# Strassen's seven block products for gate and up, and the down projection as a phase of its own, in a two-layer diffusion backbone

## Chip, cores and metric

One NeuronCore of a Trainium2 chip. The metric is the device time of one execution in microseconds (us), the median of several runs.

## What is computed

Two layers over 1024 latent tokens and 256 context tokens, width 1024. Each layer normalizes its input, mixes tokens (windowed attention, a Fourier mix, a gated linear attention), projects out, and then runs a SwiGLU feed-forward network (FFN). The change concerns the FFN of the latent tokens:

```python
def swiglu(h, w_ffn_in, w_ffn_out):
    gate, up = jnp.split(h @ w_ffn_in, 2, axis=-1)
    return (jax.nn.silu(gate) * up) @ w_ffn_out

        x = x + gt1 * (mix @ w_out[l])
        h2 = rms_norm(x, g_norm2[l]) * (1.0 + sc2) + sh2
        x = x + gt2 * swiglu(h2, w_ffn_in[l], w_ffn_out[l])
```

The hidden width is 2816, 22 inner tiles of 128 (`FT`). Everything is float32.

## The kernel before

Activations lie with features on the partitions: a `[128, 8, 512]` tile holds the 1024 features (eight blocks, `KT`) of one half of the latent tokens (half 0, half 1). To keep float32 precision at the fast matmul rate, every operand is split in a high part (a cast, ScalarE) and the rest (a subtraction, VectorE): `split`, lines 160 to 162. A product then takes three matmuls (`mm3`, lines 164 to 168: high x high, high x low, low x high), and `gemm` (lines 170 to 174) sums eight blocks in one PSUM bank: 24 matmuls of 128x512. `load_w` (line 143) loads a weight tile of 512 KB into one of two `raw` buffers and splits it into one of three `wh` and three `wl` buffers.

The code is written as generators that `weave` (line 71) runs in turn, each with its pace in `PACE`; a framework then orders each engine's queue by the order of the code and by which operands it expects to be ready, and inserts all semaphores. Loads and stores are issued from SP's queue. An engine's queue is worked off in order.

`lat_early` (line 1106) projects half 0 out, normalizes it, and in layer 1 does its first FFN blocks beside the rest of the attention; `lat_late` (line 1082) does the same for half 1. In the norm (`norm_stats` line 379, `norm_apply_g` line 401) each block of 128 features takes one VectorE step, one ScalarE step that writes the high part, and one VectorE step that writes the low part. The norm of half 1 is cut in two (`self.mid`): gate and up of half 0 of the first block stand between its statistics and its application.

The FFN (`ffn_lat`, line 1190) goes in 11 blocks of two inner tiles (`FB`). `ffn_up` makes gate and up of both halves of a block: 96 matmuls per inner tile; the gate goes through Silu (line 1125), the up result is multiplied by it (line 1138), the product is split and stays on the chip. `ffn_down` (line 1165) follows one block later: for each half and each of the eight output blocks six matmuls into one bank, whose result is scaled and added into the half's `x` (line 1178). Every inner tile's down weights are loaded and split once and used for both halves. Between the blocks of layer 0 stand seven rows each of the next layer's modulation (`next_mod`, line 1046): a row is a 512 KB load into a `raw` buffer and one VectorE multiply-and-sum (line 326). In layer 1 the first `F0` = 2 blocks of half 0 are done early, and those of half 1 at the end.

Of the kernel before, what the change touches and what calls it, by code (L numbers as in the profile page):

```python
# [8 lines left out]
F32 = mybir.dt.float32  # L9
# [14 lines left out]
F0 = 2  # L24
# [17 lines left out]
class Prog:  # L42
# [55 lines left out]
    def run(self):  # L98
# [17 lines left out]
        self.mid = None  # L116
# [47 lines left out]
    def mm3(self, ps, wh, wl, xh, xl, start, stop):  # L164
        mm = self.nc.tensor.matmul
        mm(ps, wh, xh, start=start, stop=False)  # L166
        mm(ps, wh, xl, start=False, stop=False)  # L167
        mm(ps, wl, xh, start=False, stop=stop)  # L168
# [249 lines left out]
    def layer(self, l):  # L418
# [9 lines left out]
        with tc.tile_pool(name=f"mix{l}", bufs=2, reuse_waits="tile") as mp:  # L428
# [12 lines left out]
            self.ch, self.pend, self.joint = {}, None, True  # L441
# [604 lines left out]
    def next_mod(self, l, pool):  # L1046
        nc = self.nc
        cs = {}
        for s, n in (("c", 16), ("l", 48)):
            cs[s] = self.t(pool, [128, 1024], F32, "cs", 1)  # L1050
# [10 lines left out]
    def lat_load(self, l, c, x, pool, tag):  # L1061
        act = self.act_tiles(pool, tag, 8, 2, 512)
# [4 lines left out]
        self.ch[c] = (act, x, pool, tag)  # L1067

    def lat_proj(self, l, c):
        act, x = self.ch[c][:2]  # L1070
        for m in range(KT):
# [3 lines left out]
            self.nc.vector.scalar_tensor_tensor(x(m), ps, self.mods[l, "l", 0][2][:, m:m + 1], x(m), ALU.mult, ALU.add)  # L1075
            yield 5.1

    def lat_late(self, l, x):
        self.lat_load(l, 1, x, self.fp, "H2")
        yield PACE[f"late{l}"]  # L1080
        yield from self.lat_proj(l, 1)
        yield from self.wait((l, "early"))
        if not self.f0:
            for z in range(2):
                self.prefetch("wff1", l, 0, z)
        self.mid = self.lat_norm_g(l, 1)
        next(self.mid)

    def lat_norm(self, l, c):
        for _ in self.lat_norm_g(l, c):  # L1090
            pass

    def lat_norm_g(self, l, c):
        n = 512
        _, x, pool, tag = self.ch[c]
        a2, sh2, _ = self.mods[l, "l", 1]
        h2 = self.act_tiles(pool, tag, 8, 2, n)
        nr = self.norm_stats(self.resident(x, n), n, False)
        yield
        self.norm_apply(self.resident(x, n), n, nr, a2, sh2, h2, False)  # L1100
        self.ch[c] = (h2, x)

    def lat_early(self, l, x, f0):
        self.lat_load(l, 0, x, self.bp, "H")
        yield 10
        yield from self.lat_proj(l, 0)
# [3 lines left out]
        self.lat_norm(l, 0)  # L1110
        self.emitted.add((l, "early"))
        yield 10
        if f0:
            yield from self.ffn_steps(l, [(b, [0]) for b in range(f0)], False, self.mm_ps)

    def ffn_up(self, l, b, cs, table, tag=("nx", 3)):
        nc = self.nc
        gs = {}

        def gate(c, w):  # L1120
            ps = self.mm_ps()
            self.gemm(ps, w, self.ch[c][0])
            sg = self.t(self.tp, [128, 512], F32, *tag)[:]
            if table:
                i = nc.scalar.activation(sg, ps, ACTF.Silu)
                self.last_silu = i.ins
            else:
                raw = self.t(self.tp, [128, 512], F32, *tag)[:]
                nc.scalar.copy(raw, ps)
                nc.scalar.activation(sg, ps, ACTF.Abs)  # L1130
                self.silu_tail(raw, sg)
                nc.vector.tensor_tensor(sg, raw, sg, ALU.mult)
            return sg

        def up(f, c, w, sg):
            ps = self.mm_ps()
            self.gemm(ps, w, self.ch[c][0])
            nc.vector.tensor_tensor(sg, ps, sg, ALU.mult)  # L1138
            if c == 0:
                g = self.t(self.bp, [128, 2, 512], F32R, "HC", 4)  # L1140
            else:
                g = self.t(self.fp, [128, 2, 512], F32R, "G", 4)
            self.split(sg, g[:, 0, :], g[:, 1, :])
            gs[f, c] = g

        ld = lambda f, z: self.load_w("wff1", l, b * FB + f, z)
        for f in range(FB):
            wg = ld(f, 0)
            wu = ld(f, 1)
            if not self.joint:  # L1150
                for c in cs:
                    if c and self.mid:
                        next(self.mid, None)
                        self.mid = None
                    sg = gate(c, wg)
                    up(f, c, wu, sg)
                self.joint = len(cs) > 1
            else:
                sgs = [gate(c, wg) for c in cs]
                for c, sg in zip(cs, sgs):  # L1160
                    up(f, c, wu, sg)
            yield 10.2 * len(cs)
        self.pend = (b, cs, gs)

    def ffn_down(self, l, psum):
        nc = self.nc
        b, cs, gs = self.pend
        gt2 = self.mods[l, "l", 1][2]
        w2 = [self.load_w("wff2", l, b * FB + f) for f in range(FB)]
        for c in cs:  # L1170
# [193 lines left out]
```

## Time and profile before

| | |
|---|---|
| median of 3 runs (range) | 3077.03 us (3073.91 to 3078.86) |
| profiled execution | 3071.83 us |
| its span, first to last instruction | 3069.9 us |
| mean granted TensorE clock | 0.966 |
| layer 0, first to last FFN gate or down projection | about 988 to 1722 us |
| layer 1, the same | about 2310 to 3067 us |

Times of rows are in us from the span's start, mean durations in ns. PE is TensorE, PEld its weight loads, DVE VectorE, ACT ScalarE, POOL GpSimd, SPq the queue of SP that issues DMAs. Matmuls are pipelined: the duration of one is longer than the distance of two starts. PEclk 1.00 is a granted clock of 2.4 GHz, 0.50 is 1.2 GHz. A row "x2" in a timeline is two instructions merged, from the start of the first to the end of the second.

### The profile page before, as it was taken

How to read it: one execution, taken by the hardware profiler on the slowest of the kernel's cores; microseconds unless marked ns; L12 is line 12 of the kernel's file. 1: busy time of each engine (PE TensorE's matmuls, PEld its weight loads, DVE VectorE, ACT ScalarE, POOL GpSimd, SP SyncE). 2: the span in 40 equal slices, each digit the busy share in tenths (PEclk: the TensorE clock that was granted, in tenths of full speed). 3: DMA queues.
4: the chain of work that ended last, by engine and by line, in shares of the span. 5: the costliest groups of instructions: out<-in, count | busy, mean ns of one | idle time of the engine just before them, and what ended most of it. 6: DMA issues, size and time to landing. Idle time of an engine off the chain costs nothing. (4 is left out here: it accounts for less than half of the span.)

```text
span 3069.9 us, 37102 instructions
## 1 busy us (share of the span) xinstructions
PE 2885.3 (94%) x14450; PEld 2316.7 (75%) x14450; DVE 1762.0 (57%) x2857; ACT 1137.8 (37%) x2064; POOL 79.4 (3%) x72
## 2 busy tenths in 40 slices
PE   6999997979989999999999998895999999999999
PEld 3577676868877888888888866664667888888887
DVE  4266778787766555444445677776665533334434
ACT  3356565555544211121112465454444311111111
POOL 0000100000000000000000000010100000000000
PEclk9999997989999999999999999995999999999999
DMA  7754452434562333332322434233342111111113
GB/s 249 255 159 137 117 163 72 131 100 155 182 202 93 110 120 106 103 110 96 114 85 96 154 121 145 86 121 110 107 134 90 62 55 49 48 48 48 42 63 109
DMA packets 156847, 349.35 MB, mean 114 GB/s; under 512 B 19136, under 2 KB 54720, under 8 KB 155648
## 3 DMA queue, kind: packets, MB, share of 16 engines
q1 hardware_dynamic: 156672, 346.98, 35.4%
q8 instruction: 114, 1.87, 0.2%
q14 instruction: 61, 0.50, 0.1%
HBM read 306.27 MB, written 38.02 MB: 112 GB/s over the span
## 5 line engine op out<-in xcount | busy, mean ns | idle before, releaser
L166 PE MATMUL mm<-H,wh 128*128 128x512 f32 x2080 | 821.4, 396 | 12.6 <-ACT HC L408 3.8
L167 PE MATMUL mm<-H,wh 128*128 128x512 f32 x2080 | 818.9, 395 | 1.3 <-DVE H L162 1.3
L168 PE MATMUL mm<-H,wl 128*128 128x512 f32 x2080 | 816.8, 393 | 0.9 <-DVE wl L162 0.9
L161 ACT CAST wh<-raw 128x1024 fp32r<-128x1024 f32 (+1 forms) x332 | 341.5, 1038 | 913.1 <-PE mm L167 473.9
L162 DVE TENSOR_TENSOR wl<-raw,wh 128x1024 fp32r<-128x1024 f32 (+1 forms) x332 | 401.7, 1218 | 389.7 <-ACT wh L161 382.6
L166 PEld LDWEIGHTS mm<-H,wh 128*128 128x128 f32 x2080 | 392.1, 189 | 102.1 <-issue 5.5
L167 PEld LDWEIGHTS mm<-H,wh 128*128 128x128 f32 x2080 | 392.6, 189 | 85.1 <-issue 2.6
L168 PEld LDWEIGHTS mm<-H,wl 128*128 128x128 f32 x2080 | 392.6, 189 | 85.1 <-issue 3.3
L1138 DVE TENSOR_TENSOR nx<-mm,nx 128x512 f32<-128x512 f32 x86 | 59.4, 690 | 202.1 <-PE mm L168 201.7
L166 PE MATMUL mm<-HC,wh 128*128 128x256 f32 (+1 forms) x560 | 166.3, 298 | 2.2 <-DVE dcol L795 1.4
L167 PE MATMUL mm<-HC,wh 128*128 128x256 f32 (+1 forms) x560 | 163.5, 293 | 0.9 <-DVE HC L409 0.6
L168 PE MATMUL mm<-HC,wl 128*128 128x256 f32 (+1 forms) x560 | 161.6, 290 | 0.8 <-DVE wl L162 0.8
L167 PE MATMUL f<-G,wh 128*128 128x512 f32 x352 | 136.9, 389 | 0.0
L166 PE MATMUL f<-G,wh 128*128 128x512 f32 x352 | 136.6, 389 | 0.3 <-DVE XA L1178 0.3
L168 PE MATMUL f<-G,wl 128*128 128x512 f32 x352 | 136.8, 389 | 0.0
L326 DVE CUSTOM_DVE_ANT_0 na<-raw,cs 128x1024 bf16<-128x1024 f32 x64 | 78.3, 1224 | 100.8 <-DMA raw<-wmodT 100.8
L166 PE MATMUL f<-HC,wh 128*128 128x512 f32 x336 | 131.2, 390 | 1.0 <-DVE XA L1178 1.0
L669 ACT ACTIVATE P<-S,nm 128x640 f32<-128x640 f32 (+2 forms) x144 | 104.7, 732 | 71.4 <-DVE nm L665 70.8
L167 PE MATMUL f<-HC,wh 128*128 128x512 f32 x336 | 130.8, 389 | 0.0
L168 PE MATMUL f<-HC,wl 128*128 128x512 f32 x336 | 130.6, 389 | 0.0
L691 PE MATMUL t<-ident,P 128*128 128x128 f32 x640 | 110.4, 288 | 12.1 <-DVE pt L696 4.8
L663 DVE TENSOR_REDUCE mx<-S 128x2 f32<-128x1280 f32 (+2 forms) x68 | 95.7, 1407 | 40.8 <-PE S L658 40.4
(441 smaller groups left out, 4465.0 us busy)
## 6 DMA issues: line engine op xcount, KB each, us to landing
raw<-wff SPq DMA_DIRECT2D x216, 512.0 KB, 3.3
raw<-wmodT SPq DMA_DIRECT2D x64, 512.0 KB, 3.6
raw<-wfm SPq DMA_DIRECT2D x52, 512.0 KB, 3.9
raw<-wout SPq DMA_DIRECT2D x40, 512.0 KB, 3.3
pt<-wmod SPq DMA_DIRECT2D x64, 256.0 KB, 4.5
qld<-q_l SPq DMA_DIRECT2D x64, 256.0 KB, 4.3
raw<-wtm SPq DMA_DIRECT2D x24, 416.0 KB, 3.7
wm<-wmod SPq DMA_DIRECT2D x8, 1024.0 KB, 9.6
```

What stands on the lines that cost most here:

```text
L161: self.nc.scalar.copy(hi, raw)
L162: (eng or self.nc.vector).tensor_tensor(lo, raw, hi.bitcast(F32), ALU.subtract)
L166: mm(ps, wh, xh, start=start, stop=False)
L167: mm(ps, wh, xl, start=False, stop=False)
L168: mm(ps, wl, xh, start=False, stop=stop)
L326: self.nc.vector.tensor_tensor_reduce(out=junk[:], in0=raw, in1=cs[s][:], op0=ALU.mult, op1=ALU.add, scale=1.0, scalar=0.0, accum_out=self ...
L663: nc.vector.tensor_reduce(mx[:, :nh], st[:, c0:c0 + nh * n].rearrange("p (a n) -> p a n", n=n), axis=AX.X, op=ALU.max)
L669: nc.scalar.activation(P[:, :n], st[:, c0 + z * n:c0 + (z + 1) * n], ACTF.Exp, bias=nm[:, hh:hh + 1], accum_out=sums[:, hh:hh + 1])
L691: nc.tensor.transpose(tp[:, hh * 128:(hh + 1) * 128], P[:, c:c + 128], self.ident[:])
L1138: nc.vector.tensor_tensor(sg, ps, sg, ALU.mult)
```

## The change

Gate and up of both halves of one inner tile are a 2 x 2 block product: weights G1, G2 and U1, U2 (the first and last four blocks of the inner dimension) times operands B11, B21 (half 0) and B12, B22 (half 1). `ffn_seven` makes it from seven products of four blocks each in place of eight. Five of its operand sets are sums or differences of the normalized halves, made and split once per layer (`combo`, `combos2`); five of the seven weight operands are sums made per inner tile on GpSimd and then split. The products run three ahead in weights, into four banks per tile, two banks taking a second product after the first has been read. The gated results go to DRAM (`gd`). The norm now writes a float32 tile in place and the split follows apart (`norm_raw`). The output projection's `x` goes to DRAM (`xm`) as well.

The down projection then is a phase by itself: for each half, 22 inner tiles, eight PSUM banks that collect all of them, each inner tile with a load of its weights (now once for each half) and of its gated result. In layer 0 the next layer's norm of half 0 stands behind the first three (`LAG`) inner tiles of half 1, which use six banks. `F0` counts inner tiles now: in layer 1 six are done in the plain way, half 0 early and half 1 ahead of `ffn_seven`, gate and up only. `next_mod` gives three rows after each of layer 0's tiles.

The diff, cut:

```diff
-F0 = 2
+F0 = 6
+FS = ("F", 20)
+LAG = 3
...
+    def norm_raw(self, l, x):
+        nr = self.norm_stats(self.resident(x, 512), 512, False)
+        for k in (4, 5, 6, 7, 0, 1, 2, 3):
+            nc.vector.scalar_tensor_tensor(x(k), x(k), a2[:, k:k + 1], nr, ALU.mult, ALU.mult)
+            nc.scalar.activation(x(k), x(k), ACTF.Identity, bias=sh2[:, k:k + 1])
...
+    def lat_late(self, l):
...
+        yield from self.lat_proj(l, 1, act, x)
+        yield from self.wait((l, "early"))
+        self.norm_raw(l, x)
+        self.raw1 = x
+        B = self.B
+        B["22"] = self.half(self.fp, FS)
+        for k in range(4):
+            self.split(x(k + 4), *B["22"](k))
+        if self.f0:
+            B["12"] = self.half(self.fp, FS)
+            for k in range(4):
+                self.split(x(k), *B["12"](k))
+        r = self.raw0
+        self.combo("1+", self.fp, FS, lambda k: (r(k), x(k + 4), ALU.add))
+        self.combo("4-", self.fp, FS, lambda k: (r(k + 4), r(k), ALU.subtract))
+
+    def combo(self, name, pool, tag, parts):
+        self.B[name] = self.half(pool, tag)
+        for k in range(4):
+            a, b, op = parts(k)
+            t = self.t(self.tp, [128, 512], F32, "nx", 3)[:]
+            (self.nc.vector if "+" in name else self.nc.gpsimd).tensor_tensor(t, a, b, op)
+            self.split(t, *self.B[name](k))
+
+    def combos2(self):
+        r, x = self.raw0, self.raw1
+        self.combo("3-", self.bp, ("H", 8), lambda k: (x(k), x(k + 4), ALU.subtract))
+        self.combo("7+", self.fp, FS, lambda k: (r(k + 4), x(k + 4), ALU.add))
+        for k in range(4):
+            self.nc.vector.tensor_tensor(r(k), r(k), x(k), ALU.add)
+        self.B["6+"] = self.half(self.fp, FS)
+        for k in range(4):
+            self.split(r(k), *self.B["6+"](k))
...
+    def ffn_seven(self, l, fs, fps):
...
+        def weights(i):
+            f, p = fs[i // 7], i % 7
+            if p == 0:
+                g = self.t(self.wp, [128, 1024], F32, "raw", 2)
+                u = self.t(self.bp, [128, 1024], F32, "XC", 2)
+                for z, w in ((0, g), (1, u)):
+                    nc.sync.dma_start(w[:], self.wff1[l, f, z].rearrange("p a b -> p (a b)"))
+                raws[f] = g, u
+            g, u = raws[f]
+            g1, g2, u1, u2 = g[:, 0:512], g[:, 512:1024], u[:, 0:512], u[:, 512:1024]
+            pair = [(u1, u2, ALU.add), (g1, g2, ALU.add), (g1, u2, ALU.add), u2, g1,
+                    (g2, u2, ALU.subtract), (u1, g1, ALU.subtract)][p]
+            if isinstance(pair, tuple):
+                src = self.t(self.tp, [128, 512], F32, "c1", 2)[:]
+                nc.gpsimd.tensor_tensor(src, *pair)
             else:
+                src = pair
...
+            self.split(src, w[:, 0, :], w[:, 1, :])
+            ws[i] = w
+
+        ops = ["11", "22", "1+", "4-", "3-", "7+", "6+"]
+        ev = self.t(self.bp, [128, 8, 512], F32, "XA", 1)
...
+            T1, T2, T3, T4 = [ev[:, 4 * (j % 2) + z, :] for z in range(4)]
+            for p in range(7):
+                i = 7 * j + p
+                if i + ahead < n:
+                    weights(i + ahead)
+                w, b = ws.pop(i), B[ops[p]]
+                ps = bank[(0, 1, 2, 0, 1, 2, 3)[p]]
...
+                    self.mm3(ps, w[:, 0, ks], w[:, 1, ks], xh, xl, first and k == 0, k == 3, skip)
+                if p == 0:
+                    nc.scalar.copy(T1, ps)
+                elif p == 1:
+                    tt(T2, T1, ps, ALU.add)
+                elif p == 2:
+                    tt(T3, ps, T2, ALU.subtract)
+                elif p == 3:
+                    nc.scalar.copy(T4, ps)
+                    tt(T2, T4, T2, ALU.subtract)
+                elif p == 4:
+                    self.last_silu = nc.scalar.activation(T1, ps, ACTF.Silu).ins
+                    tt(T3, ps, T3, ALU.add)
+                elif p == 5:
+                    tt(T2, ps, T2, ALU.add)
+                    self.last_silu = nc.scalar.activation(T2, T2, ACTF.Silu).ins
+                    tt(T2, T2, T4, ALU.mult)
+                    self.gate_out(f, 0, T2)
+                else:
+                    tt(T3, ps, T3, ALU.add)
+                    tt(T3, T3, T1, ALU.mult)
+                    self.gate_out(f, 1, T3)
+            yield f
+
+    def down_tiles(self, l, f, c):
+        w = self.load_w("wff2", l, f)
+        raw = self.t(self.tp, [128, 512], F32, "nx", 3)
+        self.nc.sync.dma_start(raw[:], self.gd[f, :, c * 512:(c + 1) * 512])
+        g = self.t(self.fp, [128, 2, 512], F32R, *FS)
+        self.split(raw[:], g[:, 0, :], g[:, 1, :])
+        return w, g
...
     def ffn_lat(self, l):
...
+            for f in range(f0):
+                drain(self.ffn_plain(l, f, 1, False))
+            self.combos2()
...
+            for f in self.ffn_seven(l, list(range(f0, FT)), fps):
                 if mod is not None:
-                    for _ in range(7):
+                    for _ in range(3):
                         next(mod, None)
...
+            for c in range(2):
...
+                ps = [self.t(fps, [128, 512], F32, "f", 4)[:] for _ in range(4)] + [self.mm_ps() for _ in range(2)]
+                lag = []
+                if c and not last:
+                    for f in range(LAG):
+                        lag.append((self.down_tiles(l, f, c), f))
+                        self.down_mm(ps, *lag[-1][0], f, range(6))
...
+                for f in range(len(lag), FT):
+                    self.down_mm(ps, *self.down_tiles(l, f, c), f, range(KT))
+                for m in range(KT):
+                    nc.vector.scalar_tensor_tensor(x(m), ps[m], gt2[:, m:m + 1], x(m), ALU.mult, ALU.add)
+                    nc.sync.dma_start(xo[:, m, c * n:(c + 1) * n], x(m))
```

## Rows read from the trace of the kernel before

**Rows 1.** The page, busy us (share of the span) xinstructions of each engine.

```profile
PE 2885.3 (94%) x14450; PEld 2316.7 (75%) x14450; DVE 1762.0 (57%) x2857; ACT 1137.8 (37%) x2064; POOL 79.4 (3%) x72
```

**Rows 2.** Windows over both FFNs: stretch, us, busy (x) by engine, PEclk, DMA, GB/s.

```profile
1015.00:1640.00 625.00, 623.73 (x2748) 515.25 (x2747) 304.69 (x427) 113.91 (x152) 0.00 (x0) 1.00 0.33 106
2425.00:3066.00 641.00, 641.00 (x2829) 530.39 (x2827) 251.22 (x308) 108.05 (x140) 0.00 (x0) 1.00 0.17 58
```

**Rows 3.** Timeline of TensorE, first and last of thirteen starts: start us, us.

```profile
939.73 0.39 PE L166 MATMUL mm<-H,wh 128*128 128x512 f32 x1
...
942.45 0.39 PE L166 MATMUL mm<-H,wh 128*128 128x512 f32 x1
```

**Rows 4.** Timeline of VectorE, layer 0, from late projection to FFN.

```profile
990.00 0.75 DVE L1075 SCALAR_TENSOR_TENSOR X<-mm,mod_0l,X 128x512 f32<-128x512 f32 x1 [0.76 <-PE mm L168]
...
996.75 0.69 DVE L353 SCALAR_TENSOR_TENSOR na<-na,nacc 128x512 f32<-128x512 f32 x1
...
1000.35 1.41 DVE L407 SCALAR_TENSOR_TENSOR nx<-X,a_0l,na 128x512 f32<-128x512 f32 x2
...
1010.20 0.75 DVE L409 SCALAR_TENSOR_TENSOR H<-nx,mod_0l,H 128x512 fp32r<-128x512 f32 x1
```

**Rows 5.** Windows at the start of each layer's FFN.

```profile
1005.00:1010.00 5.00, 5.00 (x23) 3.87 (x22) 5.00 (x8) 2.50 (x4) 0.00 (x0) 1.00 0.00 0
...
2405.00:2410.00 5.00, 5.00 (x23) 4.12 (x22) 2.80 (x4) 4.55 (x7) 0.00 (x0) 1.00 0.13 51
```

**Rows 6.** Timeline of VectorE, two splits back to back.

```profile
2287.22 1.29 DVE L162 TENSOR_TENSOR H<-c,H 128x512 fp32r<-128x512 f32 x2
```

**Rows 7.** Window in layer 1 before the FFN, with the lowered clock.

```profile
2300.00:2320.00 20.00, 17.59 (x65) 13.29 (x65) 16.11 (x23) 12.16 (x18) 0.00 (x0) 0.84 0.21 65
```

**Rows 8.** Timeline of VectorE, layer 1, early and late projection.

```profile
2362.90 0.75 DVE L1178 SCALAR_TENSOR_TENSOR XA<-mm,mod_1l,XA 128x512 f32<-128x512 f32 x1 [0.61 <-PE mm L168]
...
2400.98 0.75 DVE L1075 SCALAR_TENSOR_TENSOR X<-mm,mod_1l,X 128x512 f32<-128x512 f32 x1 [2.71 <-PE mm L168]
```

**Rows 9.** Timeline of ScalarE, two norm steps back to back.

```profile
998.26 1.39 ACT L408 ACTIVATE H<-nx,mod_0l 128x512 fp32r<-128x512 f32 x2 [0.36 <-DVE nx L407]
```

**Rows 10.** ScalarE groups, 1040 to 1600 us: busy us, mean ns | idle.

```profile
L161 ACT CAST wh<-raw 128x1024 fp32r<-128x1024 f32 x51 | 52.9, 1052 | 245.0 <-PE mm L167 117.9 <-PE f L167 104.1 <-DMA raw<-wff 23.0
...
L161 ACT CAST HC<-nx 128x512 fp32r<-128x512 f32 x18 | 11.2, 621 | 99.5 <-DVE nx L1138 99.5
```

**Rows 11.** Timeline of VectorE, modulation rows of layer 0.

```profile
1017.72 1.22 DVE L326 CUSTOM_DVE_ANT_0 na<-raw,cs 128x1024 bf16<-128x1024 f32 x1 [1.39 <-DMA raw<-wmodT]
1018.87 0.08 DVE L326 DVE_READ_ACCUMULATOR2_ANT mod_1c<- 128x1 f32 x1
1020.29 1.23 DVE L326 CUSTOM_DVE_ANT_0 na<-raw,cs 128x1024 bf16<-128x1024 f32 x1 [1.35 <-DMA raw<-wmodT]
```

**Rows 12.** Line 326, the modulation row: idle before it (us, times).

```profile
  DMA raw<-wmodT: 100.8, 47
```

**Rows 13.** Timeline, VectorE and GpSimd: beside each other, then apart.

```profile
367.99 1.28 POOL L592 TENSOR_TENSOR XA<-XA,XC 128x512 f32<-128x512 f32 x1 [10.13 <-DVE XA L591]
368.11 1.71 DVE L593 TENSOR_TENSOR XA<-XA,XC 128x512 f32<-128x512 f32 x1
...
1844.39 0.68 DVE L593 TENSOR_TENSOR P<-P,XC 128x512 f32<-128x512 f32 x1
```

**Rows 14.** DMA issues: count, KB each, median us to landing.

```profile
raw<-wff SPq DMA_DIRECT2D x216, 512.0 KB, 3.3
raw<-wmodT SPq DMA_DIRECT2D x64, 512.0 KB, 3.6
```

**Rows 15.** VectorE groups, 1040 to 1600 us, the same columns.

```profile
L162 DVE TENSOR_TENSOR wl<-raw,wh 128x1024 fp32r<-128x1024 f32 x51 | 61.7, 1222 | 83.2 <-ACT wh L161 83.0
```

**Rows 16.** Window at the start of the kernel.

```profile
0.00:100.00 100.00, 70.86 (x315) 37.27 (x316) 36.61 (x86) 35.99 (x77) 0.73 (x5) 0.93 0.78 253
```

**Rows 17.** Waits, 1040 to 1600 us: us, times, longest.

```profile
PEld f L166 <- DVE XA L1178: 3.0, 5, 1.0
```

More of the change, by code (lines that the diff above doesn't have):

```diff
@@ L1044, in out_ffn_ctx, with next_mod @@
         self.xcsrc = xo
-    def next_mod(self, l, pool):
+    def next_mod(self, l):
         nc = self.nc
@@ L1075, in lat_proj, with half @@
             self.nc.vector.scalar_tensor_tensor(x(m), ps, self.mods[l, "l", 0][2][:, m:m + 1], x(m), ALU.mult, ALU.add)
+            self.nc.sync.dma_start(self.xm[:, m, c * 512:(c + 1) * 512], x(m))
             yield 5.1
[L1078 to L1095, printed above, removed]
-        a2, sh2, _ = self.mods[l, "l", 1]
[L1097 to L1101, printed above, removed]
+    def norm_raw(self, l, x):
+        nc = self.nc
+        a2, sh2, _ = self.mods[l, "l", 1]
+        nr = self.norm_stats(self.resident(x, 512), 512, False)
+        for k in (4, 5, 6, 7, 0, 1, 2, 3):
+            nc.vector.scalar_tensor_tensor(x(k), x(k), a2[:, k:k + 1], nr, ALU.mult, ALU.mult)
+            nc.scalar.activation(x(k), x(k), ACTF.Identity, bias=sh2[:, k:k + 1])
+    def half(self, pool, tag):
+        hh = [self.t(pool, [128, 2, 512], F32R, *tag) for _ in range(2)]
+        hl = [self.t(pool, [128, 2, 512], F32R, *tag) for _ in range(2)]
+        return lambda k: (hh[k // 2][:, k % 2, :], hl[k // 2][:, k % 2, :])
     def lat_early(self, l, x, f0):
-        self.lat_load(l, 0, x, self.bp, "H")
+        act = self.lat_load(l, 0, x, self.bp, ("H", 8))
         yield 10
-        yield from self.lat_proj(l, 0)
+        yield from self.lat_proj(l, 0, act, x)
         if f0:
@@ L1109, in lat_early @@
                 self.prefetch("wff1", l, 0, z)
-        self.lat_norm(l, 0)
+        self.norm_raw(l, x)
+        self.raw0 = x
+        self.B["11"] = self.half(self.bp, ("H", 8))
+        if f0:
+            self.B["21"] = self.half(self.bp, ("H", 8))
+        for k in range(4):
+            self.split(x(k), *self.B["11"](k))
+        if f0:
+            for k in range(4):
+                self.split(x(k + 4), *self.B["21"](k))
         self.emitted.add((l, "early"))
         yield 10
-        if f0:
-            yield from self.ffn_steps(l, [(b, [0]) for b in range(f0)], False, self.mm_ps)
@@ L1116, in ffn_up @@
-    def ffn_up(self, l, b, cs, table, tag=("nx", 3)):
-        nc = self.nc
[L1118 to L1126, printed above, removed]
-            else:
[L1128 to L1140, printed above, removed]
-            else:
[L1142 to L1163, printed above, removed]
@@ L1222, in ffn_lat @@
-            for i, step in enumerate(steps):
-                drain(self.ffn_steps(l, [step], True, psum))
-                if last and i == nb - f0:
-                    store(0)
+            mod = None
+            if not last:
+                nrc = self.t(self.tp, [128, NC], F32, "nrc", 1)
+                nc.vector.tensor_copy(nrc[:], self.norm_stats(self.streamed(self.xcsrc, 0, NC), NC, True))
+                mod = self.next_mod(l + 1)
+            for f in self.ffn_seven(l, list(range(f0, FT)), fps):
```

163 lines of the change are left out of this document (91 added, 72 removed).

## The prediction

> **What bounds the kernel now.** I read the busy times first: TensorE is busy 94% of the span, VectorE 57%, ScalarE 37%, GpSimd 3% [rows 1]. Then the stretches: from 1015 to 1640 and from 2425 to 3066 us, nearly all of the two latent FFNs, TensorE is busy 1264.7 of 1266 us at a granted clock of 1.00, while VectorE works 556 us and ScalarE 222 us of them [rows 2]. So both FFNs cost their number of matmuls times a pitch, and the pitch is in the timeline: from 939.73 to 942.45 us twelve 128x512 matmuls start, 0.227 us each [rows 3]. Twelve is the change's unit, one block product: four inner blocks of 128, three matmuls each, **2.72 us**. A change that takes matmuls out must shorten this stage, unless another engine becomes the slower one; I look for that next.
>
> **Matmuls removed.** In a seven-product tile gate and up of both halves need 7 x 12 = 84 matmuls, before 8 x 12 = 96. Layer 0 has 22 such tiles, layer 1 has 16 (six stay plain). The down projection keeps its 24 matmuls per inner tile and half. That is 38 products: 38 x 2.72 = **-103.4 us**. The layer-1 early stage does six gate/up tiles of half 0 (288 matmuls) in place of four with one block's down projection (240). These 48 are moved, not added, into a stretch already dense from 2320 on: 0, at best a few us of holes.
>
> **Layer 0, from projection to FFN.** Before, the last late output arrives at 990.00, the reciprocal norm is done at 997.4 and the last normalized tile at 1010.9 [rows 4]; meanwhile TensorE stays busy, because gate and up of half 0 (10.9 us) stand in front [rows 5]. After, half 0 alone feeds one product, "11". Every other product waits for VectorE and ScalarE, for which the change adds: eight norm steps, 24 splits (sets 22, 1+, 4-, 3-, 7+ and 6+, four each) and 12 additions (1+, 7+ and the sum in place). Back to back a norm step costs VectorE 0.66 us, a split or an addition 0.60 (two in 1.41 and in 1.29) [rows 4, 6]. 8 x 0.66 + 36 x 0.60 = 26.9 us, so until 1024. The first product's evacuation T1 lies in tile XA, which is free only when the last of these splits has read it; and the fourth product reuses T1's bank. So TensorE can do three products of the first tile and, if their weights are ready, three of the second: 8.2 to 16.3 us of work in the 35 us after 990. Idle 19 to 27 us; some "4-" work needs half 0 only and goes early (-3), and the clock drops after idling: 0.84 over 20 us with 2.4 us of holes, 3 us lost [rows 7]. The norm of the context, moved here too, adds 3.5 us of VectorE if it gets in front. I take **+25**, bounds +10 and +40.
>
> **Layer 1, the same place.** Early work has priority and ends first (2363.6), the late projection runs alone until 2401.0, and again gate and up of half 0 cover the norm [rows 8, 5]. After, that cover is gone: half 0 has been done early. Half 1's plain gate needs set "12", which is split behind eight norm steps and set "22": 7.4 us to the reciprocal, 0.7 to the first ScalarE step, 8 x 0.67 for those steps (two in 1.39 [rows 9]), 4 x 0.6 for "22", 0.6 for the first tile of "12": 16.5 us, less one product that can be put in front, plus 2 us of lower clock. **+15**, bounds +5 and +20. The six plain tiles (6 x 10.9 = 65 us of TensorE) then cover the combinations; sets 7+ and 6+ need buffers that "12" and the raw half free at the end: **+2**, bounds 0 and +8.
>
> **The steady tile, layer 0.** TensorE needs 7 x 2.72 = 19.0 us. ScalarE: seven casts and four evacuations of 0.62, 6.8 us [rows 10]. GpSimd: five additions. VectorE: 7 splits and 8 evacuations at 0.60 = 9.0 us, and three rows of the next layer's modulation (seven per 62 us before) at 1.15 and an accumulator read of 0.08 [rows 11], 3.6: 12.6 us. Two things come on top. First, VectorE stood idle 100.8 us in front of 64 rows, for the row's load [rows 12]: 1.57 each, 4.7 us per tile. Before, nobody noticed; now evacuations and weight splits queue behind the waiting row, and TensorE waits for those. Second, GpSimd: its 128x512 addition takes 1.28 us, and a VectorE operation with two SBUF inputs beside it takes 1.71 in place of 0.68 [rows 13]: 1.03 lost per collision, at most 5.2 us per tile. All added: 22.5 us, 3.5 over the matmuls, +77 in 22 tiles. But GpSimd can work while VectorE waits for a row: 4.7 us hold 3.7 of its five additions, leaving 1.3 collisions: 12.6 + 4.7 + 1.3 = 18.6, just under 19.0, and products are prepared three ahead (8.2 us). Below: 0, since no tile can go under its matmuls. I take 0.8 us per tile, nearer the lower end as waits and collisions overlap, **+18**; bounds 0 and +77.
> The Trainium skill, page "SBUF — State Buffer", section "Who interferes with whom", speaks against putting the sums on GpSimd: it says the shared port is an exclusive lock, the second comer blocking until the first is through. By it a collision costs up to the whole 1.28, 6.4 us per tile and +103 if none hides; by the rows 5.2 and +77. The trace agrees on the kind.
> In layer 1 there are no rows: 9.0 + 5.2 = 14.2 us under 19.0, 0; every us over would cost 16.
>
> **SP's queue and the raw ring.** The gate tile g now sits in one of two raw buffers for the whole tile; the rows share the rest. A load takes 3.3 to 3.6 us to land [rows 14]; with two buffers rows follow each other every 2.6 us and more [rows 11], so a row holds a buffer 5.5. Three rows 16.5, a tile of g about 18 (3.3 and five products and the last split): 34.5 of the 2 x 19.0 us there are. It fits with little left. Behind a waiting load on SP stand the stores of both gated halves and the next g and u.
>
> **Down projection.** Per inner tile and half TensorE takes 5.44 us. Beside it: w2 cast 1.05 and split 1.22, now twice per layer instead of once, g cast 0.62 and split 0.6 [rows 6, 10, 15]: ScalarE 1.7, VectorE 1.8. Loads 768 KB, 145 GB/s; the start of the kernel shows 253 [rows 16]. Two raw buffers, held 3.3 + 1.05 + 1.22 and issue, deliver every 3.2 us. All hidden; every us over 5.44 would cost 88 of them. The 160 read-modify-writes saved per layer lay beside matmuls (longest waits for them: 3.0 us in all [rows 17]), -2. Between the halves of layer 0, three inner tiles fill six banks only, 12.2 us of matmuls that cover the next norm's 7.4; without it TensorE would wait those. Joins between the phases +1 each, four of them; the end: eight results now finish within 5.4 us and not within 10.9, so 2 MB of stores bunch, +3. Together **+5**.
>
> **Sum.** -103.4 + 25 + 15 + 2 + 18 + 5 = -38 us. The profiled execution took 3071.83 (span 3069.9), so 3033; the median of the runs, 3077.03, lies 5.2 above it: **3039**.
>
> **Rivals.** *(a) Nearly all is kept*: the tile runs at matmul pace and the two hand-overs cost their lower ends: -103.4 + 10 + 5 + 0 + 0 + 2 = -86, **2991**. For it: VectorE has half its time free in both FFNs. Against: in the hand-over of layer 0 it is already busy all of 1005 to 1010 [rows 5].
> *(b) VectorE becomes the bound of layer 0*: each row stands in front of VectorE's queue for its whole 3.6 us load, because g leaves the rows one raw buffer. 12.6 + 3 x 3.6 + 1.3 = 24.7 us per tile, +5.7 x 22 = +125 in place of 18: **3146**. It decides from 38 + 6 us more than my term, a tile of 21.8 us. For: rows already wait on their load 47 times; against: other work can be ordered in front of them.
> *(c) Break-even*: the tile at 21.5 us and the hand-overs as taken, **3077**: waits moved to VectorE give back all of the gain.
> *(d) The change does not do what it says*: the products wait on each other through shared banks, each read between its two products, one product's time per tile: -38 + 38 x 2.72 = +65, **3142**. Each reader has two products (5.4 us) for 0.7 us of work, so this is unlikely.
>
> **Chances.** Forecast (3010 to 3065) 0.47, (a) 0.24, just above the forecast 0.07, (c) 0.05, (b) 0.14, (d) 0.03. The runs before spread by 0.16%, so about 0.2% (6 us) can be told from no change. Faster 0.47 + 0.24 + 0.07 = 0.78, same 0.05, slower 0.17. Range for 8 in 10: 2990 (the lower bounds) to 3085, leaving out (b) and (d).
>
> **What would show it.** Right: 84 matmuls per tile at a pitch of 0.227, tile period 19 to 21 us in layer 0 and 19.0 in layer 1; TensorE idle some 20 us after the late projection of layer 0, some 14 in layer 1, with the clock down once each; the down phase without holes. Wrong: no holes there (a), or VectorE idle for row loads over 3 us each and TensorE waiting for weight splits (b).

## The result and the profile after

The changed kernel takes **3104.7 us** (median of four runs, 3104.48 to 3106.97), the kernel before 3075.5 in the same comparison: a ratio of **1.0101**, 95% interval 1.0079 to 1.0124. It is slower by 1%, 29 us, where 3039 was forecast. The matmuls went as they were meant to, and the time did not follow. The page after, engines' busy time as in [rows 1]:

```profile
PE 2809.1 (91%) x13994; PEld 2243.6 (72%) x13994; DVE 1936.0 (62%) x3061; ACT 1346.2 (43%) x2456; POOL 379.5 (12%) x278
```

456 matmuls fewer, 38 products of twelve. VectorE works 174 us more than before, GpSimd 300. The windows of the changed kernel show where TensorE now stands still (us, then busy time and count of PE, PEld, DVE, ACT, POOL, then PEclk, DMA share, GB/s):

```profile
980.00:1040.00 60.00, 33.46 (x106) 23.98 (x105) 56.58 (x71) 31.92 (x57) 27.59 (x17) 0.72 0.19 58
1040.00:1490.00 450.00, 414.73 (x1769) 335.09 (x1768) 347.81 (x466) 141.38 (x247) 137.60 (x99) 0.98 0.46 155
1620.00:1660.00 40.00, 13.32 (x46) 9.59 (x45) 25.00 (x41) 16.77 (x26) 0.52 (x1) 0.66 0.36 108
...
2450.00:2500.00 50.00, 33.28 (x123) 25.40 (x122) 35.54 (x47) 27.55 (x43) 7.15 (x4) 0.80 0.20 69
2545.00:2575.00 30.00, 22.50 (x94) 18.20 (x93) 25.60 (x32) 16.07 (x27) 14.74 (x10) 0.89 0.27 88
2600.00:2850.00 250.00, 250.00 (x1104) 207.05 (x1104) 131.99 (x196) 85.12 (x144) 87.45 (x60) 1.00 0.24 82
```

The loss of a window is its length less its matmuls at the full-speed pitch of 0.227 us [rows 3]. That counts idle time and a lowered clock together. In order of time: 36.0 us at the hand-over of layer 0 (60 - 106 x 0.2267), 49.0 in the 450 us of its seven-product tiles, 29.6 between the halves of its down projection, 22.1 at the hand-over of layer 1, 8.7 where its seven products begin; none in the sevens of layer 1. Together **145 us**, against 103 removed. Before, the two stretches of [rows 2] lost 1.3 us in all, and TensorE was busy at both hand-overs [rows 5].

**The hand-over of layer 0**, timeline of VectorE, to set beside [rows 4]:

```profile
988.08 0.74 DVE L1077 SCALAR_TENSOR_TENSOR F<-mm,mod_0l,F 128x512 f32<-128x512 f32 x1
...
997.61 0.86 DVE L354 SCALAR_TENSOR_TENSOR na<-na,nacc 128x512 f32<-128x512 f32 x1
...
1000.11 5.38 DVE L1087 SCALAR_TENSOR_TENSOR F<-F,a_0l,na 128x512 f32<-128x512 f32 x8
...
1017.92 4.02 DVE L163 TENSOR_TENSOR F<-nx,F 128x512 fp32r<-128x512 f32 x3
...
1033.49 2.49 DVE L163 TENSOR_TENSOR F<-XA,F 128x512 fp32r<-128x512 f32 x4
```

The norm is ready at 998.5, 1 us later than before [rows 4]. The last four splits, of set 6+, then end at 1036.0 and not at the forecast 1024: three splits beside GpSimd's differences cost 4.02 us, four undisturbed ones 2.49. TensorE meanwhile (start, us, matmul, idle before it):

```profile
998.42 0.39 PE L169 MATMUL mm<-H,wl 128*128 128x512 f32 x1
1002.83 0.79 PE L167 MATMUL f<-F,wl 128*128 128x512 f32 x1 [4.02 <-ACT F L162]
...
1006.15 0.80 PE L168 MATMUL f<-F,wl 128*128 128x512 f32 x1 [2.52 <-DVE F L163]
1006.74 0.63 PE L169 MATMUL f<-F,wl 128*128 128x512 f32 x1
1007.17 0.66 PE L167 MATMUL f<-F,wl 128*128 128x512 f32 x1
...
1031.78 0.80 PE L167 MATMUL f<-F,wh 128*128 128x512 f32 x1 [14.63 <-ACT F L162]
```

The longest stop, 14.63 us, ends when the chain of combinations hands on its next operands. After the idle time the starts are 0.43 us apart (1006.74 to 1007.17) and not 0.23: the granted clock is at its lower level of 1.2 GHz, not at 2.4, when work comes back (0.72 of full speed in the mean of the 60 us).

**The tiles.** The first silu of each tile is a clock of the tiles. Line 1247 of the changed kernel, the even tiles of layer 0 and then of layer 1 (count, min/median/max in ns, first and last start in us):

```profile
L1247 ACT ACTIVATE XA<-t x11: 590/598/599, 1056.0 to 1486.5; 128x512 f32<-128x512 f32 x11
...
L1247 ACT ACTIVATE XA<-t x8: 598/598/600, 2587.3 to 2853.9; 128x512 f32<-128x512 f32 x8
```

Layer 0: 430.5 us for 20 tiles, **21.5 each**. Layer 1: 266.6 for 14, 19.04 each, the matmuls alone. The two differ mainly by the modulation rows, which layer 1 has not. Line 327 on VectorE's timeline in layer 0, beside [rows 11]:

```profile
1204.67 2.31 DVE L327 CUSTOM_DVE_ANT_0 na<-raw,GC 128x1024 bf16<-128x1024 f32 x1
...
1213.49 1.23 DVE L327 CUSTOM_DVE_ANT_0 na<-raw,GC 128x1024 bf16<-128x1024 f32 x1 [3.50 <-DMA raw<-wmodT]
...
1218.27 2.02 DVE L327 CUSTOM_DVE_ANT_0 na<-raw,GC 128x1024 bf16<-128x1024 f32 x1 [0.42 <-DMA raw<-wmodT]
```

A row took 1.22; now 21 of the 64 take over 2, and from the eighth tile on one row per tile waits 3.5 us or more for its load. GpSimd's timeline beside these rows:

```profile
1204.22 1.67 POOL L1205 TENSOR_TENSOR c<-XC,raw 128x512 f32<-128x512 f32 x1 [1.82 <-DVE HC L163]
1210.07 1.29 POOL L1205 TENSOR_TENSOR c<-XC 128x512 f32<-128x512 f32 x1 [4.17 <-DVE HC L163]
```

The row of 1204.67 has a sum of GpSimd beside it. The next sum falls into the wait for the next row, and that row then takes 1.23. The waits of 1040 to 1490 us (engine, line, waited for: us in all, times, longest) show who waits for VectorE:

```profile
POOL c L1205 <- DVE HC L163: 96.2, 36, 6.6
DVE na L327 <- DMA raw<-wmodT: 76.0, 38, 5.4
POOL c L1205 <- DVE wl L163: 75.2, 26, 7.2
POOL c L1205 <- DVE wh L163: 61.7, 26, 6.5
...
PEld f L167 <- DVE XA L1240: 17.6, 8, 3.3
PEld t L167 <- DVE XA L1240: 16.6, 9, 2.2
```

TensorE waits for the T2 addition (line 1240) that frees a bank. GpSimd waits for VectorE's splits: its sums go into a temporary that the split of an earlier sum frees.

**Between the halves** TensorE stops for 25.9 us (its timeline; below, SP's: the loads of gated tiles):

```profile
1655.41 0.80 PE L167 MATMUL f<-F,wh 128*128 128x512 f32 x1 [25.93 <-ACT F L162]
```
```profile
1645.99 2.65 SPq L360 DMA_DIRECT2D nx<-xc  x3
1651.97 10.23 SPq L1263 DMA_DIRECT2D nx<-gd  x8
```

The gated tiles of half 1 are loaded into the same three buffers "nx" that the next layer's norm and its streamed context tiles go through, and their first load is issued at 1651.97, after the last of those.

### The profile page after: what moved, and what is told of

It reads as the page before. It is cut to its first block, busy times and chain, and to the rows that moved or that the text cites. A ratio compares the mean times of both kernels' runs of the same rounds, so it can differ in the third digit from the quotient of the medians.

```text
span 3102.5 us, 38050 instructions
## 1 busy us (share of the span) xinstructions
PE 2809.1 (91%) x13994; PEld 2243.6 (72%) x13994; DVE 1936.0 (62%) x3061; ACT 1346.2 (43%) x2456; POOL 379.5 (12%) x278
## 5 line engine op out<-in xcount | busy, mean ns | idle before, releaser
L162 ACT CAST wh<-raw 128x1024 fp32r<-128x1024 f32 (+2 forms) x303 | 309.0, 1023 | 545.1 <-PE t L168 278.5
L169 PE MATMUL mm<-H,wl 128*128 128x512 f32 x676 | 271.9, 404 | 0.0
L167 PE MATMUL mm<-H,wh 128*128 128x512 f32 x652 | 265.5, 409 | 4.1 <-ACT H L162 3.7
L168 PE MATMUL mm<-H,wh 128*128 128x512 f32 x652 | 262.1, 404 | 0.8 <-DVE H L163 0.8
L167 PE MATMUL f<-F,wh 128*128 128x512 f32 x468 | 184.8, 395 | 48.1 <-ACT F L162 48.1
L167 PE MATMUL mm<-F,wh 128*128 128x512 f32 x480 | 190.1, 396 | 19.6 <-ACT F L162 15.1
L168 PE MATMUL mm<-F,wh 128*128 128x512 f32 x480 | 190.8, 397 | 0.5 <-DVE F L163 0.5
L168 PE MATMUL f<-F,wh 128*128 128x512 f32 x468 | 184.1, 393 | 1.6 <-DVE F L163 1.6
L169 PE MATMUL f<-F,wl 128*128 128x512 f32 x468 | 184.5, 394 | 0.0
L169 PE MATMUL mm<-F,wl 128*128 128x512 f32 x456 | 180.2, 395 | 0.5 <-DVE wl L163 0.5
L167 PE MATMUL mm<-HC,wh 128*128 128x256 f32 x544 | 159.3, 294 | 1.9 <-DVE dcol L798 1.4
L168 PE MATMUL mm<-HC,wh 128*128 128x256 f32 x544 | 156.2, 288 | 0.6 <-DVE HC L410 0.3
L169 PEld LDWEIGHTS mm<-H,wl 128*128 128x128 f32 x676 | 129.7, 192 | 28.4 <-issue 2.8
L167 PEld LDWEIGHTS mm<-H,wh 128*128 128x128 f32 x652 | 124.5, 191 | 34.6 <-issue 5.5
L168 PEld LDWEIGHTS mm<-H,wh 128*128 128x128 f32 x652 | 124.5, 191 | 26.9 <-DVE H L163 1.7
```

The costliest lines, as they stand in the source:

```text
L162: self.nc.scalar.copy(hi, raw)
L167: mm(ps, wh, xh, start=start, stop=False, skip_group_check=skip)
L168: mm(ps, wh, xl, start=False, stop=False, skip_group_check=skip)
L169: mm(ps, wl, xh, start=False, stop=stop, skip_group_check=skip)
```

## The experiments

Times are medians; "changed" is the changed kernel, 3104.7. The runs of before beside them had medians of 3072.7 to 3074.2. Tile means are from the even tiles of layer 0 as above; with a cover, from the odd ones of the 19 that are left.

| run | us | ratio to before (95%) | tile, layer 0 |
|---|---|---|---|
| norm in steps | 3081.6 | 1.0024 (1.0011 to 1.0036) | 21.6 |
| rows issued early | 3116.6 | 1.0134 (1.0116 to 1.0152) | 21.1 |
| sums on VectorE | 3061.5 | 0.9955 (0.9937 to 0.9973) | 19.5 |
| three raw buffers | 3108.2 | 1.0113 (1.0098 to 1.0128) | 21.1 |
| norm and sums | 3032.7 | 0.9866 (0.9840 to 0.9892) | 19.5 |
| sums, GpSimd busy | 3142.1 | 1.0225 (1.0198 to 1.0252) | 22.5 |
| norm, sums, cover | **3006.2** | **0.9777** (0.9753 to 0.9800) | 19.7 |
| cover alone | 3074.1 | 1.0002 (0.9989 to 1.0015) | 21.7 |
| rows not loaded | 3088.5 | 1.0052 (1.0032 to 1.0073) | see there |
| more cover | 3009.1 | 0.9786 (0.9768 to 0.9803) | 19.8 |
| four plain tiles | 3014.1 | 0.9801 (0.9786 to 0.9816) | - |
| rows paced, no load | 3063.6 | 0.9963 (0.9949 to 0.9977) | 19.15 |

**The norm in steps.** The next layer's norm of half 0 is made lazily and drawn on once per tile of half 1:

```
-                    self.next_act = {"l": self.norm1(...)}
-                    self.next_act["c"] = self.norm1(...)
+                    self.next_act = {}
+                    step = self.chain(self.norm1(..., lazy=True), self.norm1(..., lazy=True))
...
                     self.down_mm(ps, *self.down_tiles(l, f, c), f, range(KT))
+                    if lag:
+                        next(step, None)
```

> The next layer's norm is no longer ordered in one piece between the first three inner tiles of half 1's down projection and the rest: one of its 16 steps follows each later tile. Theory (the norm's 16 steps stand ahead of the splits of the next tiles on VectorE and hold the buffers that the next gated tiles are loaded into; the changed kernel lost 29.5 us of matmul time at 1620 to 1660 us for that): layer 0's second down half shrinks from 151 us to about 121 to 125, the time falls by 24 to 30 us to 3075 to 3081. Rival (the loss comes from the six-bank start or the clock and is only moved): the half stays above 140 us and the time within 8 us of the changed kernel's 3104.7.

-23 us, just under the 24 to 30 expected. The window over the boundary, of this run and then of the changed kernel:

```profile
1600.00:1680.00 80.00, 79.26 (x348) 64.92 (x347) 50.84 (x68) 36.16 (x51) 0.52 (x1) 1.00 0.51 172
```
```profile
1600.00:1680.00 80.00, 53.32 (x222) 42.70 (x221) 50.77 (x74) 35.90 (x53) 0.52 (x1) 0.83 0.48 156
```

VectorE does the same 51 us of work, and TensorE no longer waits for it. The norm's place in the order was the loss; whether through VectorE's order or through the buffers "nx", this run does not tell apart.

**Rows issued early, and three raw buffers.** In the first, a row's load stands before a yield and its product after it, with one step after products 2, 4 and 6; in the second, the ring "raw" has 3 buffers in place of 2.

```
-                self.mod_row(l, s, r, self.load_raw(self.wmodT[l - 1, r]), cs)
+                raw = self.load_raw(self.wmodT[l - 1, r])
+                yield 1
+                self.mod_row(l, s, r, raw, cs)
```

> The same rows of the modulation, three per inner tile, but each row's load is issued about two products (5.4 us) before its multiply-and-sum, which is no longer the next thing in VectorE's queue. Theory (the loads at the head of VectorE's queue, some 3.5 us once per tile and up to 0.8 twice, delay the T2 add that the fifth product's bank waits for): waits of VectorE for the row DMA go from about 76 us between 1040 and 1490 us to under 20, an inner tile of layer 0 falls from 20.6 to 21.1 us to 19.0 to 19.6, the time by 25 to 40 us to 3065 to 3080. Rival A (the collisions of GpSimd's weight sums with VectorE are the cause): the waits go, the tile stays over 20.2 us, the time 3094 to 3106. Rival B (products wait for banks as such): no change, 3100 to 3108.

> A third buffer in the ring of raw weights and rows. Now two rows can be under way while the gate weights hold the third. Theory (one free buffer serialises row loads at the head of VectorE's queue): the waits of VectorE for row DMAs at 1040 to 1490 us fall from 76 us to 15 to 45, tile 19.3 to 20.2 us, time 3075 to 3095. Rival (collisions, or banks): waits may fall, the tile stays 20.4 to 21.1, time 3097 to 3108. Elsewhere in the kernel the third buffer should change little, within 5 us.

Both missed: +12 and +3.5, and the waits for rows hardly moved (70.9 and 69.6 us in place of 76.0). SP's timeline of the first tells why (the row's load still comes behind the next tile's weights; VectorE reaches the row at 1222.4 and waits 3.45 until it lands):

```profile
1219.47 0.33 SPq L1198 DMA_DIRECT2D raw<-wff  x1
1220.11 0.33 SPq L1198 DMA_DIRECT2D XC<-wff  x1
1221.28 11.79 SPq L141 DMA_DIRECT2D raw<-wmodT  x3
```

Why a third buffer did not shorten the waits was not followed. So these two did not test the waits at all. Why the first lost 12 us was not followed further than to its second tile, which comes 16 us late; its later tiles are shorter than the changed kernel's (21.1 against 21.5).

**Sums on VectorE**, and the same **with GpSimd kept busy** on sums that nobody reads:

```
-                nc.gpsimd.tensor_tensor(src, *pair)
+                nc.vector.tensor_tensor(src, *pair)
```
```
+                nc.gpsimd.tensor_tensor(self.dummy[:], *pair)
```

> The sums and differences of the weights move from GpSimd to VectorE. VectorE gets about 5 x 0.68 = 3.4 us more per inner tile and no collisions. Rival A (collisions stretch the rows from 1.22 to 1.68 us mean, and that is what delays the adds): tile of layer 0 falls to 19.0 to 19.6 us, time 3070 to 3085. Theory (waits for the row loads): rows go back to about 1.22 us each but the waits of 3.5 us stay, and what is won by the rows (3 x 0.46 = 1.4 us per tile) is less than what is added: tile 20.5 to 22 us, time 3100 to 3130; layer 1 stays at 19.04 us a tile.

> As the run with the sums on VectorE, but GpSimd still computes the same five sums per inner tile into a tile that nobody reads; no engine waits for them. It tells why moving the sums won 43 us. Collision theory (VectorE's reads of SBUF are held up while GpSimd works): the rows go back from their VectorE-alone 1.2 us to about 1.6 to 1.7 us, and of the 43 us at least half is lost again: 3085 to 3110 us. Rival (what was slow is the way of a weight block through GpSimd, which waits for the temporary, works 1.3 us and hands on to ScalarE and VectorE; collisions don't matter): stays at 3058 to 3068 us.

Here my theory of that moment fell: more work on VectorE won 43 us, and the time fell below even rival A's 3070 to 3085. With GpSimd busy again, the time went 80 us up, over the 3085 to 3110 of the collision theory; no wait of that run names the sums that nobody reads. One group of the run with the sums on VectorE, 1040 to 1490 us, gives the price of one sum there (mean 686 ns):

```profile
L1205 DVE TENSOR_TENSOR c<-raw,XC 128x512 f32<-128x512 f32 x40 | 27.4, 686 | 0.1
```

The row's group, 1060 to 1440 us (busy, mean ns, idle before), of the changed kernel, of the sums on VectorE, and with GpSimd busy:

```profile
L327 DVE CUSTOM_DVE_ANT_0 na<-raw,GC 128x1024 bf16<-128x1024 f32 x57 | 97.2, 1705 | 67.4 <-DMA raw<-wmodT 67.2
```
```profile
L327 DVE CUSTOM_DVE_ANT_0 na<-raw,GC 128x1024 bf16<-128x1024 f32 x62 | 75.8, 1223 | 54.2 <-DMA raw<-wmodT 54.2
```
```profile
L327 DVE CUSTOM_DVE_ANT_0 na<-raw,GC 128x1024 bf16<-128x1024 f32 x56 | 79.8, 1426 | 37.6 <-DMA raw<-wmodT 36.9 <-DVE wh L163 0.5
```

**Are the waits harmless, then?** Two runs take the loads away and leave out the rows' own values: first one resident row, then, to keep the pace, the buffers that the tile has just finished.

```
-                self.mod_row(l, s, r, self.load_raw(self.wmodT[l - 1, r]), cs)
+                self.mod_row(l, s, r, row[:], cs)
```
```
+                self.mod_row(l, s, r, self.evrow, cs)
...
+            self.evrow = ev[:, 4 * (j % 2) + 2:4 * (j % 2) + 4, :].rearrange("p a b -> p (a b)")
             yield f
```

> The changed kernel, but the 64 rows of the next layer's modulation are not loaded: VectorE multiplies one resident row 64 times, so that its work and GpSimd's are as in the changed kernel and the wait for the row loads is gone. It leaves out the rows' own values. Two runs before did not shorten these waits (76 us between 1040 and 1490 us became 71 and 70), so that their price is still open. Theory of waits: tile of layer 0 from 20.6 to 21.1 down to 19.0 to 19.5 us, time 3064 to 3080 us. Collision theory: the rows still take 1.6 to 1.7 us each beside GpSimd, but VectorE gets back some 3.5 us a tile; if only the collisions mattered, tile over 20.3 us and time 3092 to 3104. In between: both are needed, the queue is only too long with both.

With nothing to wait for, VectorE took all 64 rows between 1054 and 1238 us. The silu's line of that run, while rows run and after, and the window of the first:

```profile
L1249 ACT ACTIVATE XA<-t x5: 598/599/600, 1054.9 to 1238.8; 128x512 f32<-128x512 f32 x5
```
```profile
L1249 ACT ACTIVATE XA<-f x6: 597/600/600, 1257.9 to 1448.3; 128x512 f32<-128x512 f32 x6
```
```profile
1054.90:1238.80 183.90, 163.16 (x674) 131.32 (x674) 182.07 (x257) 50.81 (x88) 80.56 (x41) 0.94 0.24 85
```

183.9 us for 8 tiles with eight rows each, 23.0 a tile, and VectorE is busy 182.1 of them: here its work alone, without a wait, sets the tile. Then 190.4 for 10, 19.04, with GpSimd's sums going on. The sums alone cost nothing.

> The run without the row loads did not keep the rows' pace: with nothing to wait for, VectorE did all 64 of them in the first nine inner tiles. Here each row's multiply-and-sum reads the two buffers that the inner tile has just finished (and scales by 1e-6) instead of a loaded row, so that three come per tile as in the changed kernel, GpSimd's sums stay, and no load is waited for. It leaves out the rows' own values. If the waits for the loads cost the tile its 2 us: 19.0 to 19.6 us per tile in layer 0, time 3065 to 3080. If the collisions do: 20.3 to 21.1 us per tile, time 3090 to 3106.

-41 us: without waits, and with GpSimd still beside it, the tile is as fast. (This run also takes the rows' loads out of SP's queue and out of the ring "raw"; what each of these is worth it does not tell apart.) Neither rival as I had put it holds, since taking away either one wins nearly all. What both take from is VectorE's time, in the window 1060 to 1440 us, first the changed kernel, then the sums on VectorE, GpSimd busy, and rows paced:

```profile
1060.00:1440.00 380.00, 347.66 (x1484) 280.39 (x1482) 298.48 (x390) 113.39 (x202) 130.78 (x94) 0.98 0.46 157
```
```profile
1060.00:1440.00 380.00, 375.72 (x1642) 306.33 (x1641) 318.68 (x531) 125.57 (x220) 0.00 (x0) 1.00 0.53 174
```
```profile
1060.00:1440.00 380.00, 336.00 (x1412) 267.28 (x1410) 338.83 (x458) 105.54 (x188) 146.93 (x90) 0.97 0.46 150
```
```profile
1060.00:1440.00 380.00, 379.21 (x1672) 313.42 (x1672) 295.34 (x432) 127.94 (x218) 142.01 (x95) 1.00 0.26 90
```

84 matmuls are a tile. VectorE's busy time and its waits for rows (67.2, 54.2, 36.9, 0), per tile: (298.5 + 67.2) / 17.7 = **20.7 us**; (318.7 + 54.2) / 19.5 = **19.1**; (338.8 + 36.9) / 16.8 = **22.4**; 295.3 / 19.9 = **14.8**. The tiles took 21.5, 19.5, 22.5 and 19.15. A tile takes what TensorE needs, 19.04, or what VectorE's queue needs, whichever is longer. In the first three VectorE is idle otherwise for only 0.8, 0.4 and 0.2 us a tile, in the last for 4.2. There VectorE's work is 14.8 us where the changed kernel has 16.9, so that taking away the waits took away some of the collisions too: with idle time on VectorE, GpSimd does part of its sums in it.

**Cover for the hand-overs.** With the norm in steps and the sums on VectorE; then everything else in the kernel as it was.

```
-F0 = 6
+F0 = (3, 6)
+FE = (0, 3)
...
+            for c, fs, steps in ((0, range(self.fe, f0), self.late_norm(l)), (1, range(f0), self.late_combos(l, nrc))):
+                for q in self.plain_seq(l, list(fs), c):
+                    for _ in range(q):
+                        next(steps, None)
+                drain(steps)
```

F0 is the number of plain tiles per layer, FE how many of them run before the late projection; plain_seq gives one step of the norm or of a combination its turn after each part of a plain tile. The squares of half 1's norm follow each late result.

> Both edits that won alone: the norm in steps (-23 us against the changed kernel) and the weight sums on VectorE (-43). If the two losses are separate places, they add: 3104.7 - 23 - 43 = 3039 us, range 3033 to 3046. Rival (VectorE, now with the sums, is what both relieve, so that they overlap): 3050 to 3060.

> On top of the norm in steps and the sums on VectorE: both layers hand over under cover. The squares of half 1's norm ride with its projection; three inner tiles per layer run plainly on half 0 (layer 0 now has three plain tiles, +3 x 2.72 = 8.2 us of matmuls; layer 1 keeps six, of which three wait until here) while the norm's other steps and the first combinations go beside them one by one, and the rest beside the plain tiles of half 1. Theory (the hand-over stalls of the changed kernel, 35.6 us in layer 0 at 980 to 1040, 21 in layer 1 at 2450 to 2500 and 9 at the entry into the seven products, are VectorE's and ScalarE's chain without matmuls beside it): against the run without the cover 65 us of stalls less, 8 us of matmuls and some 10 us of stall from VectorE's length back, so -40 to -48: 2990 to 3002 us. Rival (VectorE is full there whatever is placed beside it, so the stall is only moved): -15 or less, 3025 to 3045 us.

> The cover at both hand-overs alone, on the changed kernel: the weight sums stay on GpSimd and the norm at the boundary of the halves in one piece. Theory (the hand-over is a loss of its own place): as beside the other edits, -27, and a little more since three inner tiles of layer 0 leave the slow seven: 3104.7 - 27 - 3 x 1.5 = 3073 us, range 3066 to 3082. Rival (it paid only because VectorE had been relieved of collisions): 3085 to 3100 us.

The two first edits add up (3032.7; 3038.4 by the sum of the two). The cover wins 26.6 on top of them and 30.6 alone, so the hand-over is a loss of its own place; but less than the 40 to 48 expected. The windows over both hand-overs and the sevens of layer 0, of the run with all three:

```profile
960.00:1070.00 110.00, 103.48 (x436) 82.78 (x436) 94.67 (x132) 75.55 (x127) 13.70 (x8) 0.97 0.35 115
1060.00:1440.00 380.00, 372.74 (x1628) 303.99 (x1626) 318.46 (x532) 131.36 (x232) 0.00 (x0) 1.00 0.53 175
2340.00:2480.00 140.00, 133.81 (x573) 108.64 (x572) 103.67 (x139) 80.59 (x127) 13.70 (x8) 0.98 0.34 111
```

By the same reckoning as above 11.2 and 10.1 us are still lost at the hand-overs, after 66.8 in the changed kernel. The run with norm and sums had lost 57.4 at the same places (980 to 1040, 2370 to 2420, 2475 to 2500), and not the 65 that the expectation started from. That is 36 less, of which three more plain tiles take 8.2 and the last gated tile, into which ten of the 64 rows fall, some 7. At 3006 us this version beats both kernels, by 2.2% and 3.2%.

**More cover.** The differences 4- and 3- on VectorE too and, in layer 1, half 0's squares beside its projection; then four plain tiles in layer 0 (F0 = (4, 6)):

```
-            (self.nc.vector if "+" in name else self.nc.gpsimd).tensor_tensor(t, a, b, op)
+            self.nc.vector.tensor_tensor(t, a, b, op)
```

> The best kernel so far (norm in steps, weight sums on VectorE, cover) with the differences of the activations on VectorE too, and in layer 1 the squares of half 0's norm beside its projection. The best kernel loses 7 us at 1030 to 1040, 16 us at 2250 to 2280 and 5.5 us at 2390 to 2400. Expected: half of the last two and of the first: 3006 - 12 = 2994 us, range 2986 to 3002. Rival (VectorE has no room left there): 3002 to 3008.

> The same with four plain inner tiles in layer 0 instead of three: +2.72 us of matmuls for 10.9 us more of cover in either half. If VectorE is what the first hand-over still waits for, the stall of 7 us goes and the time is 2 to 5 us below the run with three; if the stall has already gone, it is 2 to 3 us above.

Nothing won: +3, which is within the spread of the runs (3004.7 to 3013.0 against 3001.0 to 3008.4), and +8. The same two windows of the first:

```profile
960.00:1070.00 110.00, 106.31 (x457) 84.97 (x457) 95.50 (x147) 76.05 (x130) 0.00 (x0) 1.00 0.37 123
2340.00:2480.00 140.00, 136.90 (x589) 111.04 (x588) 103.33 (x150) 81.04 (x129) 0.00 (x0) 0.99 0.35 116
```

The hand-overs now lose 6.4 and 6.5 us in place of 11.2 and 10.1, so VectorE still had room there, against the rival. But from the end of layer 0's down projection to the last late result of layer 1, the stretch with the other half of this edit, the trace is 11 us longer (662.2 to 672.9); why was not followed. The fourth plain tile made layer 0, from the last late result to the end of the FFN, 3.6 us longer (689.8 to 693.4) for 2.7 us of matmuls.

## Why the prediction was wrong

**Right:** the matmuls (456 removed, [rows 1] against the page after), the sevens of layer 1 at matmul pace (19.04), the down projection's tiles, which run without holes outside the boundary (TensorE is busy all of 1490 to 1620 and of 1660 to 1760), and the places of three stalls.

**"Between the halves of layer 0, three inner tiles fill six banks only, 12.2 us of matmuls that cover the next norm's 7.4"**: priced within +5, it cost 29.6, and undoing it alone won 23. The six banks were not what counted: the run that won 23 still starts with them. The three tiles could not run ahead at all, because their loads stand behind the norm: eight latent and eight context steps use the three "nx" buffers first. I had counted the reciprocal norm's 7.4 us and neither the 16 steps nor the ring that both need.

**"The steady tile, layer 0", +18**: it cost 49. The failed step is "GpSimd can work while VectorE waits for a row: 4.7 us hold 3.7 of its five additions, leaving 1.3 collisions". The waits were near the forecast, 67.2 / 17.7 = 3.8 us a tile. But GpSimd works in them far less than reckoned. Of its 94 sums between 1060 and 1440 us, counted in the rows of both engines, 17 lie for more than half in such a wait: one per tile, where 3.7 had been put. GpSimd is at work in 26.9 of the 67.4 us of waits. The likely reason is in the 233 us of waits in three rows above: the next sum needs a temporary that a split on VectorE frees, and a VectorE that waits for a row makes no split. (Where GpSimd's sums wait for no temporary, in the run that keeps it busy, it fills 29.5 of 37.6 us.) Most of the other sums run beside VectorE.

VectorE's work per tile is 298.5 / 17.7 = 16.9 us; undisturbed it is 318.7 / 19.5 - 5 x 0.69 = 12.9, by the run with the sums on VectorE. So 4.0 of the 5.2 us of possible collisions came true, and not 1.3. 16.9 + 3.8 = 20.7, over the 19.04, where 18.6 had been reckoned to be under it; VectorE's other idle time, 0.8, makes up the 21.5. VectorE is the bound of layer 0, as rival (b) has it, but by another sum: one row per tile waits long for its load, not three, the collisions make up for the rest, and TensorE waits for the T2 addition, not for weight splits. The tile's length is that of rival (c), 21.5, just short of the 21.8 from which (b) was to be told.

The Trainium skill, page "SBUF — State Buffer", section "Who interferes with whom", has the second comer at the shared port wait until the first is through. The rows above agree: the sum of 1204.22 has 1.22 us to go when the row of 1204.67 starts, and that row takes 2.31 in place of 1.22.

**"Layer 0, from projection to FFN", +25**: 36, inside its bounds. TensorE's idle time in the 60 us, 26.5, is within the 19 to 27 forecast; the lower clock was under-priced, at some 9 us (33.46 busy for 106 matmuls that take 24.0 at the full pitch) where 3 had been taken. VectorE's list was right, its pace not: it ended at 1036, not 1024, for the most part because of the same collisions, now with the differences 4- and 3- on GpSimd. **"Layer 1, the same place", +15**: 22, over its upper bound of 20. The chain took what had been costed, 16.0 us from the last late result to the first plain gate (16.5 forecast); but no product stood in front of it, for which 2.7 had been taken off, and the lower clock cost some 5 us (33.28 busy for 123 matmuls, 27.9 at the full pitch) and not 2. **The entry into the seven products, +2**: 8.7, over 8; its cause was not followed.

**The sum.** From the last late result to the end of the FFN, layer 0 went from 732.7 to 774.9 us and layer 1 from 668.9 to 645.3, with 59.9 and 54.4 us of matmuls less (22 products; 16 products and the 48 matmuls moved). That is 102 + 31 = 133 us of loss where the terms came to 65. (The five windows above hold 145; the kernel before had lost some 15 in the same two stretches itself.) The profiled spans differ by 32.6 us; of the 14 that lie ahead of layer 1's late projection the 48 moved matmuls make 10.9. All five terms erred to the same side: the chains were costed with VectorE nearly undisturbed, with buffers free and with the clock hardly lowered.

## What to carry to other kernels

Where TensorE's work is cut, add up for each stage what every other engine's queue needs per tile, its waits for loads and its stretched operations included, and compare that sum with the new time of the matmuls: it sets the tile as soon as it is longer. Work that stands in one piece between two dense phases (a norm, a set of combinations) is best cut into steps and dealt out beside matmuls, and for each tile loaded ahead it is worth asking whose earlier tiles must leave its buffers first. An engine that helps should be priced with what it does to the one that it relieves: here five sums per tile cost less on the busier engine.

## What had not been expected of the hardware

A 128x1024 multiply-and-sum on VectorE takes 1.22 us alone and up to 2.31 beside one GpSimd addition, and GpSimd's own additions grow with it, from 1.28 [rows 13] to 1.70 in the mean for one of their forms. GpSimd's groups of the changed kernel, 1040 to 1490 us (busy, mean ns, idle before):

```profile
L1205 POOL TENSOR_TENSOR c<-XC,raw 128x512 f32<-128x512 f32 x20 | 34.1, 1704 | 33.4 <-DVE HC L163 14.9 <-DVE wl L163 11.2 <-DVE wh L163 7.4
...
L1205 POOL TENSOR_TENSOR c<-raw 128x512 f32<-128x512 f32 x20 | 25.7, 1287 | 121.6 <-DMA raw<-wff 37.6 <-DVE HC L163 37.0 <-DVE wh L163 21.7
```

The same five additions per tile, for which no other engine waited, made the kernel 80 us slower (3061.5 to 3142.1). In layer 0 they raised VectorE's work per tile by 3.8 us (318.7 / 19.5 to 338.8 / 16.8), more than the 5 x 0.69 = 3.4 that the five need on VectorE itself.
